# GpSimd takes over loads from SyncE, and two steps move behind the value weights

## The chip, the cores and the metric

One core of one Trainium2 chip. The metric is the device time of one execution in microseconds (us). Engines: TensorE (PE), VectorE (DVE), ScalarE (ACT), GpSimd (POOL), and SyncE (SP), which only issues DMAs. ACT and POOL issue DMAs too, each on a queue of its own. An engine runs its instructions in the order in which they were put on it; one that waits holds all that stand behind it.

## What is computed

One step of a hybrid decoder layer for 2048 prompt tokens and 8 samples of one token each, all in float32, with a width of 1024:

```python
ada = silu(c) @ w_ada + b_ada;  shift, scale, gate = split(ada, 3)
hn = rmsnorm(x, g_norm) * (1 + scale) + shift
xa, za, q, k, v, glr, zg = split(hn @ w_in)           # 5136 columns in all
# RG-LRU group: conv4 over xa, block-diagonal gates, linear recurrence h, y_lru = h * silu(za)
# GLA group, 4 heads, DK 128, DV 256:
log_alpha = log_sigmoid(glr @ w_gla_g2 + b_gla_g2) / 16
S_t = diag(alpha_t) S_{t-1} + k_t^T v_t;  o_t = q_t S_t      # for samples: from state_gla
y_gla = rmsnorm(o) * g_gla_norm * silu(zg)
x = x + gate * (concat(y_lru, y_gla) @ w_out);  y = rmsnorm(x, g_final)
```

Outputs are y for prompt and samples and the new states.

## The kernel before

The prompt is worked in two halves of 1024 tokens; the samples ride with the second half as 8 more columns. Each float32 operand is split into a high and a low part (`hi`, `lo`; `hh`, `hl` for hn), and a product is three matmuls: hi by hi, hi by lo, lo by hi. `hh` and `hl` hold hn transposed, 1024 features on 8 x 128 partitions, for one half at a time.

**hn of the second half.** `modulate` (L187) is called eight times per pair of token tiles, from a list of small steps (`drips`) that the projections of the first half's last tile call between matmuls. Each call turns two k-tiles on PE, scales and shifts the two halves out of PSUM on ACT (L199, L200), rounds on POOL (`hh`, L201) and subtracts on DVE (`hl`, L202). g is the group of 256 tokens, 0 to 3.

**Seven products.** The gates of three heads and two pairs of LRU columns of the second half are made by a Strassen-like scheme with seven products (`seven`, L1517), in the order ZB11, ZT1, ZT2, ZB22, ZT3, ZB21, ZT4. `sums` (L1440) makes their operands out of hn with long DVE steps. To make room, a quarter of hn (the first four k-tiles, second 512 tokens: `a21`, L1437) is overwritten, and kept in DRAM in `a21d`. L1622 loads it back after the last product. The silu of the gates goes to DRAM (`zgd`).

**The heads of the second half.** `gla_head(1, h)` (L1134) runs for h = 3, 0, 1, 2, each followed by one LRU tile:
- `value_weights` (L321) loads two halves of the value weights, in a pool of three places of 1 MB (tag `w`): already split, from `parts` in DRAM (L302), and raw (tag `wr`, two places, L293), because the samples' values use the raw ones.
- `values` (L910): with `sample_values` (L881) first: 64 small matmuls with 8 columns as weights (L889), four copies out of PSUM (L893, to `vs`) and four stores to `vsd` (L896). Then eight token tiles of 24 matmuls (`value_mm`, L335 to L337), each in one of four PSUM places (`acc`). In the first head the 16 low-rank columns ride along, and their transposes wait in the list `turns`; at three entries the oldest is run.
- weights of k and q, also from `parts`, projections (`project`, L650 to L652), the decay, and the chunks of the attention, which are put off by counts of units (`after`, `tick`) and run between the projections.
- `sample_state` (L1055), twice with four samples: loads the samples' values (`vb`, from `vsd`, L1062) and old states (`s0`, L1064) into two places (tag `xt`), scales on ACT (L1068), adds on DVE (L1069); `sample_out` makes the outputs on PE (L1078) and stores the new states (L1079). The normed samples' output `os` goes through PE at L1128.
- `gate_load` (L1165) loads the gates of one segment from `zgd` into `zs` (four places); `finish` uses them (L1131).

Beside this, POOL's queue carries the preparation of the output weights: loads `r` (L806), stores `wd`, `wd2` (L841, L834), whose arithmetic is put on DVE and ACT between other work.

**Who decides the order.** Where the code says `in_order`, the instructions of all engines but SP keep the program's order. Elsewhere the builder puts them on each engine by when they can run by its own reckoning, with the program's order as priority. So SP's issues, and PE's matmuls in `values`, need not follow the program.

Of the kernel before, what the change touches and what calls it, by code (L numbers as in the profile page):

```python
# [8 lines left out]
F32 = mybir.dt.float32  # L9
F32R = mybir.dt.float32r  # L10
I32 = mybir.dt.int32
AF = mybir.ActivationFunctionType
OP = mybir.AluOpType

P = 128
# [4 lines left out]
NS = 8  # L20
H = 4
DK = 128
DV = 256
# [15 lines left out]
HEADS = (3, 0, 1, 2)  # L39
# [10 lines left out]
def dram(ap, off, pattern):  # L50
    return bass.AP(tensor=ap.tensor, offset=ap.offset + off, ap=pattern)
# [3 lines left out]
def hybrid_kernel(ctx, tc, i, o):  # L55
    nc = tc.nc
    V, S, G, PE, SP = nc.vector, nc.scalar, nc.gpsimd, nc.tensor, nc.sync
# [13 lines left out]
    vsd = dpool.tile([H, NS, DV], F32, tag="vsd", name="vsd")  # L71
# [5 lines left out]
    zgd = dpool.tile([8, P, TH + NS], F32, tag="zgd", name="zgd")  # L77
    a21d = dpool.tile([2, P, 4, 512], F32, tag="a21d", name="a21d")
# [32 lines left out]
    Gm = cp.tile([P, KT, 9], F32, name="Gm")  # L111
    Sh = cp.tile([P, KT, 9], F32, name="Sh")
# [74 lines left out]
    def modulate(xt, g, kts):  # L187

        c = slice(g * 256, (g + 1) * 256)
        for k2 in range(kts[0], kts[1], 2):  # L190
            pt = tps().rearrange("p (k t) -> p k t", k=2)
            cg = slice(g % 2 * 256, g % 2 * 256 + 256)
            f = (fs4[(1, 2, 0)[k2 // 4 if g < 2 else 2]][:, k2 % 4:k2 % 4 + 2, cg] if g < 2 or k2 >= 4
                 else ra[k2 // 2][:, :, cg])
            for kt in range(2):
                for j in range(2):
                    PE.transpose(pt[:, kt, j * P:(j + 1) * P],
                                 xt[j][:, (k2 + kt) * P:(k2 + kt + 1) * P], ident)
            S.activation(f[:, 0], pt[:, 0], AF.Identity, scale=Gm[:, k2, 8:9], bias=Sh[:, k2, 8:9])  # L199
            S.activation(f[:, 1], pt[:, 1], AF.Identity, scale=Gm[:, k2 + 1, 8:9], bias=Sh[:, k2 + 1, 8:9])  # L200
            G.tensor_scalar(hh[:, k2:k2 + 2, c], f, 1.0, 0.0, op0=OP.mult, op1=OP.add)  # L201
            V.tensor_tensor(hl[:, k2:k2 + 2, c], f, hh[:, k2:k2 + 2, c].bitcast(F32), op=OP.subtract)  # L202

# [70 lines left out]
    parts = {}  # L274
# [4 lines left out]
    def weights(col, n, k0=0, nk=KT, samples=False, both=None, later=False, pieces=1):  # L279


        q = 48 if n == DV else 0
        c = slice(q, q + nk * n)
        if both is None:
            both = wp.tile([P, 2, 1088], F32R, tag="w", name="w", bufs=3)
        hi, lo = [both[:, j, c].rearrange("p (k n) -> p k n", n=n) for j in range(2)]
        known = (col, k0) in parts
        raw = None
        if samples or not known:
            raw = wp.tile([P, 1088], F32, tag="wr", name="wr")[:, :nk * n].rearrange("p (k n) -> p k n", n=n)  # L290
            for k in range(0, nk, nk // pieces):
                r = slice(k, k + nk // pieces)
                load = lambda r=r: SP.dma_start(raw[:, r], i["w_in"][  # L293
                    0, (k0 + r.start) * P:(k0 + r.stop) * P, col:col + n].rearrange("(k p) n -> p k n", p=P))
                loads.append(load) if k else load()
        split = []
        for k in range(0, nk, nk // pieces):
            r = slice(k, k + nk // pieces)
            split += [lambda r=r: S.copy(hi[:, r], raw[:, r]),
                      lambda r=r: V.tensor_tensor(lo[:, r], raw[:, r], hi[:, r].bitcast(F32), op=OP.subtract)]  # L300
        if known:
            SP.dma_start(both[:, :, c].bitcast(F32), parts[col, k0])  # L302
        else:
            splits.extend(split)
            if not later:
                split_parts()
            parts[col, k0] = dpool.tile([P, 2, nk * n], F32, tag=f"w{col}_{k0}", name="parts")
            stores.append((parts[col, k0], both[:, :, c].bitcast(F32)))
            if not later:
                store_parts()  # L310
        return hi, lo, raw
# [9 lines left out]
    def value_weights(h, samples):  # L321
        n = DV + (RANK if h == HEADS[0] else 0)
        return [weights(V0 + h * DV, n, k0, 4, samples) for k0 in (0, 4)]
# [4 lines left out]
    def drip():  # L328
        if drips:
            drips.pop(0)()  # L330
# [95 lines left out]
    with tc.tile_pool(name="ada", bufs=1, side="right") as ap:  # L426
# [79 lines left out]
        with in_order():  # L506
# [13 lines left out]
            pt = turn(xt0[0:2], (0, 1))  # L520
# [10 lines left out]
            for c in range(1, 4):  # L531
                k = (2 * c, 2 * c + 1)
                if c > 1:
                    ada(c, (0, KT))
                pt = [turn(xt0, (kt,)) for kt in k]
# [345 lines left out]
    def sample_values(h, w, n):  # L881

        n4 = n // 4
        vs = gp.tile([P, DV], F32, tag="os", name="vs")
        ps = acc()
        for kt in range(KT):
            raw = w[kt // 4][2]
            for g in range(4):
                PE.matmul(ps[32 * g:32 * g + NS, :n4], fs[:, kt], raw[:, kt % 4, g * n4:(g + 1) * n4],  # L889
                          start=kt == 0, stop=kt == KT - 1)  # L890
        for g in range(4):
            r = slice(32 * g, 32 * g + NS)
            (S.copy if g % 2 else V.tensor_copy)(vs[r, :min(n4, DV - g * n4)], ps[r, :min(n4, DV - g * n4)])  # L893
        for g in range(4):
            c = slice(g * n4, min((g + 1) * n4, DV))
            G.dma_start(vsd[h][:, c], vs[32 * g:32 * g + NS, :c.stop - c.start])  # L896
        if n > DV:
            r = slice(96, 96 + NS)
            return low_rank(ps[r, DV - 3 * n4:n4], r, TH)
        return lambda: None  # L900
# [9 lines left out]
    def values(half, h, w):  # L910
        first = h == HEADS[0]
        n = DV + (RANK if first else 0)
        vh, vl = new_values()
        turns = [sample_values(h, w, n)] if half == 1 else []
        for tt in range(8):
            if tt == 4:
                while drips:
                    drip()
            c = slice(tt * P, (tt + 1) * P)
            ps = acc()  # L920
            value_mm(ps[:, :n], c, w, n, (0, KT))
            hi, lo = vh[tt // 4][:, tt % 4], vl[tt // 4][:, tt % 4]
            S.copy(hi, ps[:, :DV])  # L923
            V.tensor_tensor(lo, ps[:, :DV], hi.bitcast(F32), op=OP.subtract)  # L924
            if len(turns) == 3 or tt == 7 and turns:
                turns.pop(0)()
            if first:
                turns.append(low_rank(ps[:, DV:n], slice(0, P), tt * P))
            tick(0.5)
        for f in turns:  # L930
            after(1, f, True)
        return vh, vl
# [122 lines left out]
    def sample_state(h, smp, b0, st, done):  # L1055

        if b0 == 0:
            st[:] = [cp.tile([P, NS, 32], F32, tag="sc", name="qm"), gp.tile([P, DV], F32, tag="os", name="os")]
            V.memset(st[0], 0.0)
        qm = st[0]  # L1060
        vb = xp.tile([P, 4, DV], F32, tag="xt", name="xt")
        SP.dma_start(vb, dram(vsd, (h * NS + b0) * DV, [[0, P], [DV, 4], [1, DV]]))  # L1062
        s0 = xp.tile([P, 4, DV], F32, tag="xt", name="xt")
        SP.dma_start(s0, i["state_gla"][0, b0:b0 + 4, h].rearrange("b k v -> k b v"))  # L1064
        for n in range(4):
            b = b0 + n
            V.tensor_copy(qm[:, b, b:b + 1], smp[:, 0, b:b + 1])
            S.activation(s0[:, n], s0[:, n], AF.Copy, scale=smp[:, 2, b:b + 1])  # L1068
            V.scalar_tensor_tensor(s0[:, n], vb[:, n], smp[:, 1, b:b + 1], s0[:, n],  # L1069
                                   op0=OP.mult, op1=OP.add)  # L1070
        after(3, lambda: sample_out(h, b0, st, s0, done), True)
# [62 lines left out]
    def gla_head(half, h, wv=None):  # L1134
        ns = len(SEGS[half])
        if wv:
            wk, wq = wkq0
            v, prep0, rest = first_head()
        else:
            v = values(half, h, value_weights(h, half == 1))  # L1140
            wk = weights(K0 + h * DK, DK)
            wq = weights(Q0 + h * DK, DK)
        prep, zs, os_, state = {}, {}, [None], []
# [21 lines left out]
        def gate_load(s):  # L1165
            c0, n = SEGS[half][s]
            for dt in range(2):
                z = new_zs()
                SP.dma_start(z[:, :n], zgd[2 * h + dt][:, c0:c0 + n])
                zs[s, dt] = z[:, :n]  # L1170

        def finish(s):
# [264 lines left out]
    def a21():  # L1437
        return [(hh, hl)[u][:, :4, 512:TH] for u in range(2)]
# [180 lines left out]
        gates_seven(1 + n)  # L1619
    while drips:  # L1620
        drip()
    for u, x in enumerate(a21()):  # L1622
        SP.dma_start(x.bitcast(F32), a21d[u])
    close_sp()
    for k, h in enumerate(HEADS):
        gla_head(1, h)
# [282 lines left out]
    for x in pairs[:2]:  # L1909
        x.new(A11)  # L1910
        r = wp.tile([P, 1088], F32, tag="wr", name="wr")[:, :D].rearrange("p (q k t) -> p q k t", q=2, k=4)
# [214 lines left out]
    for n in range(2, 16):  # L2126
        g = n - 1
# [17 lines left out]
    for q in range(8):  # L2145
        g, k = 2 + q // 2, q % 2
# [63 lines left out]
```

## Time and profile before

| | us |
|---|---|
| runs | 1469.28, 1469.33, 1471.35 |
| median | 1469.33 |
| profiled execution | 1468.39 |
| its span, first to last instruction | 1466.6 |

| engine | busy us | share |
|---|---|---|
| PE | 1428.5 | 97% |
| DVE | 1049.6 | 72% |
| ACT | 690.0 | 47% |
| POOL | 188.7 | 13% |

Times in rows are us from the span's start. hn of the second half is made from about 560 to 603, the seven products run from about 602 to 710, the heads of the second half from 710 to about 1090, then LRU tiles and, to the end, the output projection. A row of a timeline has start, duration, engine, line, operation, tiles written and read, shape, count, and in brackets the idle time of the engine ahead of it with what ended it; of a row with a count it is the first of the merged ones. SPq and ACTq are DMA issues of SP and ACT. A row of waits has who waited for what, total us, times, longest.

### The profile page before, as it was taken

To read this page: it belongs to the slowest core of one execution; us is meant where nothing else is said; L and a number is where in the kernel's file an instruction comes from. 1 tells how busy PE (TensorE), PEld (TensorE's weight loads), DVE (VectorE), ACT (ScalarE), POOL (GpSimd) and SP (SyncE) were. 2 spreads that over 40 slices of the span, in tenths; PEclk is the share of its full clock that TensorE was granted. 3 is DMA by queue.
4 is the path that set the end of the run, shared out by engine and by line. 5 is a ranking of instruction groups with operands and counts; after the bars stand their busy time and mean duration, and the time that the engine had idled before them with its cause. 6 is when DMAs were issued, how large, how long until landed. Compare 5 with 4: busy or idle time off the path is not lost.

```text
span 1466.6 us, 23589 instructions
## 1 busy us (share of the span) xinstructions
PE 1428.5 (97%) x8741; PEld 1254.4 (86%) x8741; DVE 1049.6 (72%) x2473; ACT 690.0 (47%) x1255; POOL 188.7 (13%) x316
## 2 busy tenths in 40 slices
PE   8999999999999999999999899999999999999998
PEld 6888988899898988788899899999998887778886
DVE  5757657776666778845458678586778986688886
ACT  4653544652445467624353454534557622144342
POOL 1200111212121121100102222222100000000000
PEclk9999999999999999999999999999999999999999
DMA  9755876765656455657836746567353757693453
GB/s 331 259 183 176 272 243 214 255 213 184 202 197 219 127 192 196 225 194 247 313 107 202 244 151 196 181 207 256 130 201 104 277 200 266 251 360 122 139 177 115
DMA packets 169944, 305.33 MB, mean 208 GB/s; under 512 B 12962, under 2 KB 102722, under 8 KB 167389
## 3 DMA queue, kind: packets, MB, share of 16 engines
q1 hardware_dynamic: 119029, 233.21, 47.0%
q0 software_dynamic: 17888, 53.56, 10.4%
q10 hardware_dynamic: 32912, 17.04, 3.8%
q8 instruction: 69, 1.13, 0.3%
q14 instruction: 46, 0.38, 0.1%
HBM read 188.51 MB, written 115.33 MB: 207 GB/s over the span
## 4 chain that ended last, share of the span: by engine, by line
PE 76%; DVE 8%; DMA 6%; ACT 5%; issue 5%; POOL 1%; SPq 0%; ACTq 0%; DVEq 0%; POOLq 0%
PE acc L1797 12%; PE acc L650 10%; PE acc L651 10%; PE acc L652 10%; PE tp L1797 9%; PE acc L1511 6%; PE acc L335 3%; PE acc L336 3%; PE acc L337 3%; DMA w<-parts 2%; PE po L1040 1%; DMA mixd<-zs 1%; PE acc L1271 1%; PE tp L1126 1%; PE acc L1273 1%
## 5 line engine op out<-in xcount | busy, mean ns | idle before, releaser
L650 PE MATMUL acc<-hh,w 128*128 128x512 f32 (+3 forms) x1112 | 386.9, 348 | 6.5 <-DMA w<-parts 5.4
L651 PE MATMUL acc<-hl,w 128*128 128x512 f32 (+3 forms) x1112 | 376.4, 338 | 0.0
L652 PE MATMUL acc<-hh,w 128*128 128x512 f32 (+3 forms) x1112 | 375.9, 338 | 0.0
L650 PEld LDWEIGHTS acc<-hh,w 128*128 128x128 f32 x1112 | 209.8, 189 | 25.1 <-DVE e L985 3.6
L651 PEld LDWEIGHTS acc<-hl,w 128*128 128x128 f32 x1112 | 209.9, 189 | 17.9 <-issue 1.2
L652 PEld LDWEIGHTS acc<-hh,w 128*128 128x128 f32 x1112 | 209.7, 189 | 16.3
L1797 PE MATMUL acc<-w,a 128*128 128x512 f32 (+1 forms) x792 | 184.8, 387 | 0.0
L1797 PEld LDWEIGHTS acc<-w,a 128*128 128x128 f32 x792 | 146.8, 188 | 33.2 <-issue 3.4
L335 PE MATMUL acc<-w,hh 128*128 128x256 f32 (+1 forms) x508 | 145.5, 286 | 4.9 <-DMA w<-parts 3.1
L337 PE MATMUL acc<-w,hl 128*128 128x256 f32 (+1 forms) x508 | 143.4, 282 | 0.0
L336 PE MATMUL acc<-w,hh 128*128 128x256 f32 (+1 forms) x508 | 143.3, 282 | 0.0
L1797 PE MATMUL tp<-w,a 128*128 128x512 f32 x564 | 136.0, 391 | 0.0
L1797 PEld LDWEIGHTS tp<-w,a 128*128 128x128 f32 x564 | 105.3, 188 | 26.8 <-issue 5.1
L335 PEld LDWEIGHTS acc<-w,hh 128*128 128x128 f32 x508 | 96.3, 190 | 7.4 <-DMA w<-parts 3.3
L337 PEld LDWEIGHTS acc<-w,hl 128*128 128x128 f32 x508 | 96.7, 190 | 0.0
L336 PEld LDWEIGHTS acc<-w,hh 128*128 128x128 f32 x508 | 96.2, 189 | 0.1
L1092 ACT ACTIVATE zs<-acc 128x512 f32<-128x512 f32 (+3 forms) x71 | 34.7, 488 | 107.7 <-PE acc L652 97.4
L1647 ACT CAST a<-s 128x512 fp32r<-128x512 f32 x61 | 36.5, 620 | 96.0 <-issue 36.7
L1234 DVE SCALAR_TENSOR_TENSOR cv<-xa,vecT,cv 128x512 f32<-128x512 f32 (+2 forms) x120 | 76.3, 639 | 7.0 <-ACT cv L1232 6.5
L1093 DVE SCALAR_TENSOR_TENSOR zs<-zs,acc 128x512 f32<-128x512 f32 (+3 forms) x71 | 38.9, 548 | 46.4 <-ACT zs L1092 46.4
L923 ACT CAST vh<-acc 128x256 fp32r<-128x256 f32 x56 | 20.7, 371 | 89.4 <-PE acc L337 74.0
L924 DVE TENSOR_TENSOR vl<-acc,vh 128x256 fp32r<-128x256 f32 x56 | 23.2, 421 | 51.5 <-ACT vh L923 51.2
(393 smaller groups left out, 2721.5 us busy)
## 6 DMA issues: line engine op xcount, KB each, us to landing
parts<-w SPq DMA_DIRECT2D x37, 1024.0 KB
w<-parts SPq DMA_DIRECT2D x28, 1024.0 KB
wr<-in_w_in_dram SPq DMA_DIRECT2D x44, 512.0 KB
a<-mixd SPq DMA_DIRECT2D x63, 256.0 KB
w<-wd SPq DMA_DIRECT2D x12, 1024.0 KB
w<-twd SPq DMA_DIRECT2D x20, 512.0 KB
mixd<-zs ACTq DMA_DIRECT2D x34, 256.0 KB
wada<-in_w_ada_dram SPq DMA_DIRECT2D x16, 512.0 KB
```

Source lines behind the costliest of these rows:

```text
L335: PE.matmul(ps, hh[:, kt, c], hi[:, kt % 4], start=kt == 0, stop=False)
L336: PE.matmul(ps, hh[:, kt, c], lo[:, kt % 4], start=False, stop=False)
L337: PE.matmul(ps, hl[:, kt, c], hi[:, kt % 4], start=False, stop=kt == KT - 1)
L650: PE.matmul(ps[:, :n], hi[:, kt], a, start=kt == 0, stop=False)
L651: PE.matmul(ps[:, :n], hi[:, kt], b, start=False, stop=False)
L652: PE.matmul(ps[:, :n], lo[:, kt], a, start=False, stop=kt == KT - 1)
L1092: S.activation(z, ps, AF.Tanh, scale=0.5)
L1093: V.scalar_tensor_tensor(z, z, 1.0, ps, op0=OP.add, op1=OP.mult)
L1234: V.scalar_tensor_tensor(cv[:, cq], xa[:, cq.start + k:cq.stop + k], cw[k], cv[:, cq], op0=OP.mult, op1=OP.add)
L1511: PE.matmul(ps, w[:, u, k], x[v][k], start=start and (k, u, v) == (0, 0, 0), stop=(k, u) == (3, 1), skip_group_check=True)
L1647: S.copy(t[:, 0, k], (low(t) if src is None else src)[:, k])
L1797: PE.matmul(ps, t[:, u, k], w[:, v, k, c], start=(q < 3 or ps is own) and (k, u, v) == (0, 0, 0), stop=(k, u) == (3, 1), skip_group_check= ...
```

## The change

- `modulate`: for g of 2 and 3 the second of the two activations out of PSUM is a `tensor_scalar` on DVE.
- `weights`: where the split weights lie in DRAM already, their load comes first in the program, and the raw weights' loads are issued by POOL.
- `values`: `sample_values` is called after four token tiles, not ahead of the first; `turns` is emptied down to two entries each time.
- `sample_state` and `gate_load`: their three loads are issued by POOL.
- The loads of `a21d` stand behind those of the first head's value weights.

```diff
@@ modulate
             S.activation(f[:, 0], pt[:, 0], AF.Identity, scale=Gm[:, k2, 8:9], bias=Sh[:, k2, 8:9])
-            S.activation(f[:, 1], pt[:, 1], AF.Identity, scale=Gm[:, k2 + 1, 8:9], bias=Sh[:, k2 + 1, 8:9])
+            if g < 2:
+                S.activation(f[:, 1], pt[:, 1], AF.Identity, scale=Gm[:, k2 + 1, 8:9], bias=Sh[:, k2 + 1, 8:9])
+            else:
+                V.tensor_scalar(f[:, 1], pt[:, 1], Gm[:, k2 + 1, 8:9], Sh[:, k2 + 1, 8:9], op0=OP.mult, op1=OP.add)
@@ weights
         raw = None
+        if known:
+            SP.dma_start(both[:, :, c].bitcast(F32), parts[col, k0])
         if samples or not known:
...
-                load = lambda r=r: SP.dma_start(raw[:, r], i["w_in"][
+                load = lambda r=r: (G if known else SP).dma_start(raw[:, r], i["w_in"][
                     0, (k0 + r.start) * P:(k0 + r.stop) * P, col:col + n].rearrange("(k p) n -> p k n", p=P))
...
-        if known:
-            SP.dma_start(both[:, :, c].bitcast(F32), parts[col, k0])
-        else:
+        if not known:
             splits.extend(split)
@@ values
-        turns = [sample_values(h, w, n)] if half == 1 else []
+        turns = []
         for tt in range(8):
             if tt == 4:
                 while drips:
                     drip()
+                if half == 1:
+                    turns.append(sample_values(h, w, n))
...
-            if len(turns) == 3 or tt == 7 and turns:
+            while len(turns) >= 3:
+                turns.pop(0)()
+            if tt == 7 and turns:
                 turns.pop(0)()
@@ sample_state
-        SP.dma_start(vb, dram(vsd, (h * NS + b0) * DV, [[0, P], [DV, 4], [1, DV]]))
+        G.dma_start(vb, dram(vsd, (h * NS + b0) * DV, [[0, P], [DV, 4], [1, DV]]))
         s0 = xp.tile([P, 4, DV], F32, tag="xt", name="xt")
-        SP.dma_start(s0, i["state_gla"][0, b0:b0 + 4, h].rearrange("b k v -> k b v"))
+        G.dma_start(s0, i["state_gla"][0, b0:b0 + 4, h].rearrange("b k v -> k b v"))
@@ gla_head
-            v = values(half, h, value_weights(h, half == 1))
+            w = value_weights(h, half == 1)
+            if half and h == HEADS[0]:
+                for u, x in enumerate(a21()):
+                    SP.dma_start(x.bitcast(F32), a21d[u])
+            v = values(half, h, w)
@@ gate_load
-                SP.dma_start(z[:, :n], zgd[2 * h + dt][:, c0:c0 + n])
+                G.dma_start(z[:, :n], zgd[2 * h + dt][:, c0:c0 + n])
@@ hybrid_kernel, ahead of the second half's heads
-    for u, x in enumerate(a21()):
-        SP.dma_start(x.bitcast(F32), a21d[u])
     close_sp()
```

## The prediction

> **What bounds the kernel now.** I read the page first, then the waits of TensorE (PE), then timelines and stretches around each wait that the diff can reach.
>
> ```profile
> PE 1428.5 (97%) x8741; PEld 1254.4 (86%) x8741; DVE 1049.6 (72%) x2473; ACT 690.0 (47%) x1255; POOL 188.7 (13%) x316
> ```
>
> PE is busy for 97% of the span, so an edit that leaves PE's own work as it is can gain only from PE's idle time. The diff leaves PE's matmuls as they are: it moves the samples' 64 small ones, and removes none. GpSimd (POOL) has room: 13%. The waits of PE between 690 and 1110 us, where the second half's heads run, longest first:
>
> ```profile
> PE acc L650 <- DMA w<-parts: 5.4, 2, 3.3
> PE acc L335 <- DMA w<-parts: 3.1, 1, 3.1
> PE acc L1271 <- ACT tx L1274: 2.4, 1, 2.4
> PE tp L1128 <- DVE os L1088: 2.3, 2, 1.5
> PE acc L335 <- ACT vs L893: 1.5, 1, 1.5
> ```
>
> And in the stage before them, where hn of the second half is made and the sums for the seven products begin:
>
> ```profile
> PE acc L1511 <- DVE zs L1093: 1.5, 1, 1.5
> PE acc L1511 <- DVE so L1449: 1.2, 1, 1.2
> ```
>
> Weights that arrive late cost 8.5 us in three waits, samples' values that leave PSUM late 1.5, late sample outputs 2.3, VectorE (DVE) 2.7. These are what the diff can win or make longer. A long wait costs more than itself. The stretches:
>
> ```profile
> 600.00:620.00 20.00, 17.67 (x75) 13.33 (x73) 20.00 (x21) 10.39 (x13) 1.54 (x2) 1.00 0.66 213
> 716.00:719.40 3.40, 0.29 (x4) 0.08 (x2) 0.68 (x4) 0.40 (x2) 3.09 (x6) 1.00 0.99 398
> 719.40:723.00 3.60, 3.60 (x17) 3.60 (x18) 0.34 (x1) 0.37 (x1) 1.45 (x2) 0.54 1.07 374
> 820.00:832.00 12.00, 12.00 (x107) 12.00 (x106) 5.58 (x17) 1.61 (x5) 5.26 (x9) 1.00 0.84 259
> 832.00:840.00 8.00, 4.68 (x27) 4.39 (x26) 5.49 (x15) 5.60 (x9) 0.16 (x1) 0.95 0.95 327
> 931.60:935.00 3.40, 3.01 (x17) 3.04 (x18) 2.34 (x6) 1.40 (x3) 1.57 (x3) 1.00 0.82 324
> ```
>
> The columns are the stretch, its length, the busy time of PE, weight load, DVE, ScalarE (ACT) and POOL, the granted clock, the DMA share and GB/s. After the 3.1 us wait the clock is 0.54 for 3.6 us, so that wait costs another 3.6 x 0.46 = 1.7. The shorter of the two L650 waits (5.4 - 3.3 = 2.1) ended at about 932, and the clock after it is 1.00. So between 2.1 and 3.1 us of idling lies the point from which 1.7 us more are due. [...]
>
> **The change part by part.** Durations are of the profiled execution (1468.39 us, its span 1466.6); the median shown is 1469.33, 0.94 above, and I carry the sum to it unchanged.
>
> *modulate: for g of 2 and 3 the second activation goes from ACT to DVE.* The last but one of the eight calls:
>
> ```profile
> 594.52 0.55 ACT L199 ACTIVATE fs<-tp,Sh,Gm 128x256 f32<-128x256 f32 x1
> 594.97 1.23 ACT L1281 ACTIVATE tg<-tg,lc 128x1024 f32<-128x1024 f32 x1
> 596.11 0.55 ACT L200 ACTIVATE fs<-tp,Sh,Gm 128x256 f32<-128x256 f32 x1
> ```
> ```profile
> 596.81 0.62 POOL L201 TENSOR_SCALAR hh<-fs 128x512 fp32r<-128x512 f32 x1 [3.83 <-ACT fs L200]
> ```
> ```profile
> 597.46 0.69 DVE L202 TENSOR_TENSOR hl<-fs,hh 128x512 fp32r<-128x512 f32 x1 [2.62 <-POOL hh L201]
> ```
>
> The first half is ready at 595.1, the second only at 596.7, because ACT does other work between them; DVE idles 2.62 us for it. The same operation on DVE stands in the trace once:
>
> ```profile
> L237 DVE TENSOR_SCALAR hnf<-tp,Gm,Sh x2: 544/544/545, 16.0 to 17.2; 128x256 f32<-128x256 f32 x2
> ```
>
> Eight of these are 4.4 us of DVE and take 8 x 0.55 = 4.4 from ACT. Here the second half would be done inside DVE's idle 2.62, POOL would start at about 595.2, and L202 at about 595.9: 1.5 us sooner, with the last call's 0.54 also done in the hole. From there DVE is the bound (busy 20.00 of 20.00 between 600 and 620), and PE waits for it 1.5 + 1.2 us. So DVE's lead reaches PE: 1.5 at most; 0.55 if DVE's next step waits for ACT, whose queue has lost one L200 of 0.55 there; a loss of up to 0.5 if an added operation lands on the full stretch. I take 1.3, nearer to the upper end, since the other seven holes of one call also shrink. **-1.3.** Next in line is DVE itself.
>
> *Samples' values behind four tiles.* The three non-first heads take their samples' matmuls while outputs of the head before are still pending, so the copies out of PSUM (L893) come late; in the last head a value tile waits 1.5 us for that bank. Four tiles later no such work is pending, and the wait goes. What is late next there is the query weights, below. **-1.5**, between -1.7 with the restart and 0 if the copies wait for something else. In the first head the samples also hold one of the four acc banks:
>
> ```profile
> 709.91 1.13 PE L889 MATMUL acc<-wr,fs 128*8 128x68 f32 x64
> ```
> ```profile
> 714.50 0.39 PE L335 MATMUL acc<-w,hh 128*128 128x272 f32 x1 [0.24 <-DVE zq L1093]
> ```
>
> The third tile's first half (714.50 to 716) is the last thing PE can do before the 3.1 us wait. With the samples gone a fourth tile's first half, 1.5 us, goes ahead of the wait in place of 1.1. **-0.4**, between -0.4 and +1.1.
>
> *hn's spilled part (a21d) behind the value weights; value weights before the raw ones; raw ones on POOL.* SP's issues:
>
> ```profile
> 700.57 0.32 SPq L302 DMA_DIRECT2D w<-parts  x1
> 700.94 0.43 SPq L293 DMA_DIRECT2D wr<-in_w_in_dram  x1
> 704.58 0.53 SPq L1623 DMA_DIRECT2D hh<-a21d  x1
> 705.16 0.71 SPq L1623 DMA_DIRECT2D hl<-a21d  x1
> 707.29 0.33 SPq L302 DMA_DIRECT2D w<-parts  x1
> ```
>
> In the program the a21d loads stand ahead of all the others, yet they are issued after two of them: SP's order is that in which places come free, not the program's. The a21d loads wait for the third to last product of the last seven (ZT3), the second value weights for a w buffer that the product after it (ZB21) frees. Moving the lines does not alter which is free first, so I expect a21d still at about 704.6, ahead of the weights on the same queue, and the 3.1 us wait with its 1.7 to stay. The DMA engines are full there (share 0.99 and 1.07), so a raw load on another queue changes little: **0**.
>
> *Query weights (L650's waits).* For the second head:
>
> ```profile
> 807.55 0.94 SPq L293 DMA_DIRECT2D wr<-in_w_in_dram  x2
> ...
> 819.49 0.32 SPq L1062 DMA_DIRECT2D xt<-vsd  x1
> 819.90 0.38 SPq L1064 DMA_DIRECT2D xt<-in_state_gla_dram  x1
> 827.38 4.08 SPq L1169 DMA_DIRECT2D zs<-zgd  x3
> 831.55 1.19 SPq L302 DMA_DIRECT2D w<-parts  x2
> ```
>
> The weights leave at 831.55 when the value tiles free a buffer, so an emptier SP does not bring them forward: 0 from SP's relief. If POOL's queue had bandwidth of its own, the last two gates (zs) would no longer stand in front of them: 0.39 MB by their shapes, 1.2 us at 327 GB/s in each of two heads, -2.4. [...] I keep **0**; the other side is the second rival.
>
> *Samples' states and gates on POOL.* The last head's chain has no slack:
>
> ```profile
> 1075.04 0.38 SPq L1064 DMA_DIRECT2D xt<-in_state_gla_dram  x1
> ```
> ```profile
> 1079.99 1.71 ACT L1068 ACTIVATE xt<-xt,smp 128x256 f32<-128x256 f32 x4 [5.27 <-DMA xt<-in_state_gla_dram]
> ```
> ```profile
> 1082.32 0.64 PE L1078 MATMUL po<-xt,qm 128*32 128x256 f32 x8
> ```
> ```profile
> w<-parts SPq DMA_DIRECT2D x28, 1024.0 KB
> wr<-in_w_in_dram SPq DMA_DIRECT2D x44, 512.0 KB
> ...
> out_dram<-xt POOLq DMA_DIRECT2D x8, 512.0 KB, 5.5
> ```
>
> From SP the 512 KB take 4.95 us to their reader, ACT is held for 5.27, and everything behind it on ACT waits. POOL's 512 KB transfers of the same tile land after 5.5 (median), 0.55 more, and PE's wait for os grows by that: **+0.5**, between 0 and +3 (three heads with a chain like it, and POOL held by an older store). The gates' waits inside 827.38's 4.08 us would hold POOL instead of SP, and with it samples' values, stores of the output weights and their next loads; those are used many us later, so 0; without that cover up to 4.
>
> The sum is -1.3 - 1.5 - 0.4 + 0.5 = -2.7: 1465.7 for the profiled execution, **1466.6** for the median, just inside 0.2% (2.9 us), which is about what a measurement of this kernel can tell from no change.
>
> **The rivals.** *First: a21d does go behind the second value weights.* For it: the lines are moved, and both are issued within 2.7 us. Against it: the order by readiness above. The 2 MB would no longer stand in front, the wait of 3.1 and its 1.7 go: 1466.6 - 4.8 = 1461.8.
>
> *Second, slower: next loads collide with the query weights.* The samples' matmuls end four tiles later, about 11 us, so what hangs on them moves too: the next head's two raw loads (1 MB, now at 807.55, in an easy stretch) and the samples' own two (1 MB, now at 819.5). They would fall between 820 and 835, where the share is already 0.84 and then 0.95, and the query weights are issued at 831.55. It decides once 1 MB of it is in transit at that moment: 1 MB at 327 GB/s is 3.2 us later, in the second and the third head (the last loads no raw weights ahead), and the 2.1 us wait grows past the point of the clock: 2 x 3.2 + 1.7 = 8.1, so 1474.7. For it: the shares. Against it: the stretch 820 to 832 still has room for about 0.7 MB, and weights have a queue to themselves.
>
> *Third: the gains do not arrive.* DVE's added work fills the hole without a lead, and the copies of L893 wait elsewhere: about 0 with the +0.5, so 1469.8.
>
> **How the numbers follow.** The forecast has 0.42; its terms' bounds spread it over faster 0.19, same 0.19, slower 0.04. The first rival 0.18, all faster. The second 0.27: slower 0.25, same 0.02. The third 0.13: faster 0.05, same 0.04, slower 0.04. Together faster 0.42, same 0.25, slower 0.33. The range runs from just below the first rival, 1460.5, to just above the second, 1475, with no more than 2 in 10 outside. The forecast's own range is 1464.5 to 1469.5.
>
> **What would show it.** DVE's hole before L202 at about 595 is gone, and PE's two waits at L1511 are shorter by 1 to 1.5 in sum. No wait of L335 for L893. SP still issues a21d ahead of the second value weights, and L335's wait for w<-parts stays near 3 us with a clock near 0.5 behind it; if a21d is issued later and the wait is gone, the first rival holds. L650's waits for w<-parts stay at 5.4 in two places; if they are 10 or more, the second holds. ACT's waits for the states grow by about half a us each. I am wrong if a new wait of PE appears that hangs on POOL's queue, such as gates or output weights that come late.

## The result: slower by 2 us, and the profile after

| kernel | median us | lowest to highest | executions |
|---|---|---|---|
| before, same chip | 1471.66 | 1468.40 to 1475.67 | 12 |
| changed | 1474.17 | 1469.34 to 1476.91 | 12 |

The ratio is 1.0014, with a 95% interval from 1.0000 to 1.0028: +2.1 us by the ratio, +2.5 by the medians, where the forecast said -2.7. The interval begins at no change, so this run alone shows little more than that the gain is not there. The profiled execution took 1472.66, its span 1470.9 (before: 1466.6). Lines of the changed kernel stand 3 to 11 higher than before: L653 to L655 are the projections that were L650 to L652, L338 to L340 the value matmuls, L1522 the seven products.

The page's first part. PE is as full as it was, GpSimd fuller:

```profile
PE 1431.4 (97%) x8741; PEld 1257.5 (85%) x8741; DVE 1053.5 (72%) x2481; ACT 687.5 (47%) x1247; POOL 218.8 (15%) x364
```

PE's waits between 690 and 1110 us (line, releaser: total, times, longest):

```profile
PE acc L653 <- DVE r L830: 3.7, 1, 3.7
PE acc L653 <- DMA w<-parts: 3.5, 2, 2.1
PE tp L1135 <- DVE os L1095: 2.7, 4, 1.1
PE acc L338 <- DMA w<-parts: 2.3, 1, 2.3
```

The value tile's wait for the samples' copy (1.5) is gone; the first head's wait is 2.3 (was 3.1). The key and query weights are waited for in three heads: 1.4, 3.7 and 2.1 (were 3.3, 2.1 and 0.7). The one of 3.7 is put down to another releaser (`r`), as is the 0.7 of before (`f`). But in each of the two the matmul starts 0.14 us after the last piece of the weights has landed (930.89 and 931.03; 1022.92 and 1023.06), as it does where the wait is named `w<-parts` (839.37 and 839.51 in before), so both are waits for weights.

PE's waits between 575 and 625 us:

```profile
PE tp L197 <- DVE ra L203: 3.1, 2, 2.6
PE acc L1522 <- DVE so L1460: 1.2, 1, 1.2
PE acc L1522 <- DVE ra L1460: 1.0, 1, 1.0
```

The sums are waited for 2.2 us (were 2.7), but the turned tiles, whose release has moved to DVE (L203), 3.1 (were 2.5, released by ACT):

```profile
PE tp L197 <- ACT ra L200: 2.5, 1, 2.5
```

**A ledger by stage.** All kernels here have 8741 matmuls, so the start of PE's matmul number 3500, 4000 and so on gives each stage's length (to some 0.3 us, since a few matmuls change places). "First" and "second head" here are the first and second that are worked, and a second profile of the same kernel is called "again". In the first profile of before: matmul 3500 at 556 us, 4000 at 659, 4500 at 745 (end of the first head's values), 5250 at 849, 6000 at 950, 6750 at 1049, 8500 at 1408. Differences from that profile in us:

| kernel, profile | hn, sums 3500-4000 | products, first values -4500 | second head -5250 | third -6000 | last -6750 | behind -8500 |
|---|---|---|---|---|---|---|
| before, again | +1.1 | -0.1 | -0.1 | -0.2 | +1.3 | +0.9 |
| changed | +1.9 | -1.3 | -3.0 | +4.7 | +2.3 | +0.2 |
| modulate's part alone | +1.7 | +1.1 | +0.1 | -0.3 | +1.6 | +1.3 |
| changed without modulate's part | 0.0 | -1.2 | -3.3 | +4.8 | +2.2 | -0.4 |
| ... raw weights pinned | 0.0 | -1.3 | -3.0 | +4.8 | +1.4 | -0.3 |
| ... and states held back | +1.1 | -1.4 | -2.3 | -1.2 | +4.3 | -1.0 |
| the same, again | 0.0 | -1.3 | -2.4 | -1.5 | +1.0 | -0.4 |

So the changed kernel lost in hn and in the third and last head, and won in the first and second. Two questions follow: what modulate's part costs, and what moved the weights' waits.

### The profile page after: what moved, and what is told of

It is laid out like the page before. It is cut to its first block, busy times and chain, and to the rows that moved or that the text cites. A ratio compares the mean times of both kernels' runs of the same rounds, so it can differ in the third digit from the quotient of the medians.

```text
span 1470.9 us, 23571 instructions
## 1 busy us (share of the span) xinstructions
PE 1431.4 (97%) x8741; PEld 1257.5 (85%) x8741; DVE 1053.5 (72%) x2481; ACT 687.5 (47%) x1247; POOL 218.8 (15%) x364
## 5 line engine op out<-in xcount | busy, mean ns | idle before, releaser
L653 PE MATMUL acc<-hh,w 128*128 128x512 f32 (+3 forms) x1112 | 388.7, 350 | 7.3 <-DVE r L830 3.7
L655 PE MATMUL acc<-hh,w 128*128 128x512 f32 (+3 forms) x1112 | 377.6, 340 | 0.0
L653 PEld LDWEIGHTS acc<-hh,w 128*128 128x128 f32 x1112 | 211.6, 190 | 25.6 <-DVE r L830 3.9
L655 PEld LDWEIGHTS acc<-hh,w 128*128 128x128 f32 x1112 | 211.4, 190 | 16.3
L338 PE MATMUL acc<-w,hh 128*128 128x256 f32 (+1 forms) x508 | 145.4, 286 | 2.4 <-DMA w<-parts 2.3
L340 PE MATMUL acc<-w,hl 128*128 128x256 f32 (+1 forms) x508 | 143.6, 283 | 0.2 <-DVE hl L228 0.2
L338 PEld LDWEIGHTS acc<-w,hh 128*128 128x128 f32 x508 | 96.3, 190 | 4.3 <-DMA w<-parts 2.5
L340 PEld LDWEIGHTS acc<-w,hl 128*128 128x128 f32 x508 | 96.8, 190 | 0.4 <-DVE hl L228 0.4
```

Source lines behind the costliest of these rows:

```text
L338: PE.matmul(ps, hh[:, kt, c], hi[:, kt % 4], start=kt == 0, stop=False)
L340: PE.matmul(ps, hl[:, kt, c], hi[:, kt % 4], start=False, stop=kt == KT - 1)
L653: PE.matmul(ps[:, :n], hi[:, kt], a, start=kt == 0, stop=False)
L655: PE.matmul(ps[:, :n], lo[:, kt], a, start=False, stop=kt == KT - 1)
```

## Experiments: modulate

**The part alone, and the changed kernel without it.** The first adds these lines to the kernel before, the second takes them out of the changed kernel (`...`, here and below: code left out).

```
+            if g < 2:
+                S.activation(f[:, 1], pt[:, 1], ...)
+            else:
+                V.tensor_scalar(f[:, 1], pt[:, 1], ...)
```

> The kernel before with one part of the change alone: modulate's second activation on DVE for g of 2 and 3. Collision theory (the changed kernel loses because the samples' next loads, moved four token tiles later, run beside the key and query weights of the third and the last head): nothing is moved there, so 1471.7 as the kernel before, within 1.5 either way, and key-weight waits of 5.4 us in two places. Modulate theory (the changed kernel loses in the hn stage, where PE is 2.9 us later at 600 us than at 580): the whole loss of the hn stage stands here, 1471.7 + 2.4 = 1474.1, with a PE wait of 2.6 us or more in front of L197 and a clock below 1 behind it. Chance theory (the restart of the clock comes and goes by itself): within 1 us of the kernel before.

> The changed kernel without one part: modulate's second activation on ACT again. Collision theory: 1474.2, within 1 us, key-weight waits as in the changed kernel (7 us in three places). Modulate theory: 1474.2 - 2.4 = 1471.8, PE no later at 600 us than the kernel before.

The part alone took 1475.52 against 1471.47, ratio 1.0028 (1.0019 to 1.0037). The changed kernel without it took 1472.22, ratio 1.0004 (0.9994 to 1.0014). So modulate's part alone costs 4.1 us by the ratio, clear of noise. Taken out of the changed kernel it is worth 1.5 (1.0014 to 1.0004), and there the two intervals overlap; all other parts together (+0.6) cannot be told from no change. The mechanism shows in the timelines of the changed kernel, DVE and GpSimd, 589 to 593 us:

```profile
589.12 0.69 DVE L205 TENSOR_TENSOR hl<-fs,hh 128x512 fp32r<-128x512 f32 x1 [0.48 <-POOL hh L204]
589.73 0.54 DVE L203 TENSOR_SCALAR fs<-tp,Gm,Sh 128x256 f32<-128x256 f32 x1
591.07 0.69 DVE L205 TENSOR_TENSOR hl<-fs,hh 128x512 fp32r<-128x512 f32 x1 [0.81 <-POOL hh L204]
591.68 0.54 DVE L203 TENSOR_SCALAR ra<-tp,Gm,Sh 128x256 f32<-128x256 f32 x1
```
```profile
590.42 0.62 POOL L204 TENSOR_SCALAR hh<-fs 128x512 fp32r<-128x512 f32 x1 [1.34 <-DVE fs L203]
592.37 0.62 POOL L204 TENSOR_SCALAR hh<-ra 128x512 fp32r<-128x512 f32 x1 [1.34 <-DVE ra L203]
```

Each L203 stands on DVE behind the L205 of the call before, which waits for GpSimd's L204, which waits for the L203 before it: a loop over two engines of 1.95 us a call. In the kernel before, where ACT makes both halves, the calls come in pairs, 3.25 us apart, 1.6 a call:

```profile
588.56 0.69 DVE L202 TENSOR_TENSOR hl<-fs,hh 128x512 fp32r<-128x512 f32 x1 [1.44 <-POOL hh L201]
591.81 0.69 DVE L202 TENSOR_TENSOR hl<-ra,hh 128x512 fp32r<-128x512 f32 x1 [1.36 <-POOL hh L201]
```

The tile in PSUM is held until L203 has read it, so PE turns the last call's tiles later:

```profile
592.38 0.27 PE L197 MATMUL tp<-ident,xst 128*128 128x128 f32 x1
```
```profile
594.23 0.33 PE L197 MATMUL tp<-ident,xst 128*128 128x128 f32 x1 [0.47 <-DVE ra L203]
```

The first is before, the second the changed kernel, 1.85 us later. Only the 0.47 of the wait belongs to the loop: the tiles of the call ahead are 1.22 late already (593.16, before 591.94), and from 585 to 592 PE was busy throughout, at a mean clock of 0.76. Such a slow clock comes and goes in kernels with ACT as well (last section). The profile of the part alone, with a clock of 1.00 there, shows the loop without it, with a wait of 1.30 and the tile 2.34 later than before:

```profile
594.72 0.33 PE L197 MATMUL tp<-ident,xst 128*128 128x128 f32 x1 [1.30 <-DVE ra L203]
```

**The subtraction behind the next call's activation.**

```
-            V.tensor_tensor(hl[...], f, hh[...], op=OP.subtract)
+            while rests:
+                with behind(V):
+                    rests.pop()()
+            rests.append(lambda: V.tensor_tensor(hl[...], f, hh[...], op=OP.subtract))
+            if g < 2 or k2 == 6:
+                rests.pop()()
```

> Modulate's part alone as in the first run, but with the subtraction of one call queued on VectorE behind the activation of the next call (within each g). Loop theory: the chain is cut, tp banks come free as early as with ACT, the loss of 2.6 at 600 us goes: 1471.5 or up to 1.3 below. Load theory: the same work is on VectorE, so 1475 as in the first run.

The waits of the turned tiles in the run with the part alone, and then the waits of this run, 575 to 630 us:

```profile
PE tp L197 <- DVE ra L203: 3.9, 3, 2.4
```
```profile
PE tp L199 <- DVE ra L205: 2.4, 1, 2.4
PE acc L1521 <- DVE so L1459: 1.2, 1, 1.2
PE acc L1521 <- DVE ra L1459: 1.0, 1, 1.0
```

Two of the three waits are gone and the stage is 0.6 us shorter than before (it was 1.7 longer), both with a clock of 1.00 there: the loop is what lengthened it. But the median was 1475.73 against 1471.34, ratio 1.0024 (1.0006 to 1.0042). The stage's loss went, the kernel's did not.

**DVE in the last two calls alone** (`if g < 3 or k2 < 4` for ACT).

> The kernel before with VectorE's activation in the last two calls of modulate alone (g of 3, k2 of 4 and 6), where VectorE had its hole of 2.62 us. Loop theory (with all eight calls on VectorE each call's activation waits in VectorE's queue behind the subtraction of the call before, which waits for GpSimd, which waits for the activation before: 1.95 us a call, and the tp banks come free late): two calls at the end make no such chain for PE, the hole is filled: 1471.5 - 1.0 = 1470.5, PE not later at 600 us than the kernel before. Load theory (VectorE is full between 600 and 620, and each added operation of 0.54 stands there): 1471.5 + 1.0 = 1472.5.

1472.88 against 1471.34, ratio 1.0016 (1.0002 to 1.0030), its stage 0.4 us longer. The promised gain did not come; if anything it is a loss. Two waits for the sums (L1514 for `so`) were 2.8 in total, about what before has (2.7): filling DVE's hole gave PE nothing. DVE begins its first long step of the sums at 596.47 (598.18 before), but the last call's subtraction now stands behind that step, and the next step of the sums begins only at 599.94 (600.47): most of the lead is spent on DVE itself.

**The same three on a quieter kernel.** With the states held back (next section, 1465.74) executions of one kernel scatter less (1464.44 to 1467.59).

> The kernel with the states held back until the query weights have landed, and modulate's part added as the change has it, on all eight calls. There the spread from the heads is small (1464.4 to 1467.6), so the price of that part alone shows. Loop theory: what its own stage lost, 2.0, and no more: 1465.7 + 2.0 = 1467.7. If DVE in modulate also costs some 2.4 behind its stage, as the swapped order did here (1468.1 against 1465.7): 1465.7 + 4.4 = 1470.1.

> As the run before it, with modulate's part put back in the order of the run with the subtraction behind the next activation. If the swapped order wins 0.6 us in its stage and nothing else follows from it: 0.6 below that run. If a kernel with VectorE in modulate loses 3 us behind that stage, as that run's median said and its trace did not: 3 above.

> As the run before it, with VectorE in the last two calls of modulate alone. Loop theory: 1465.7, within 0.7, or up to 1.0 below. If any use of VectorE there costs 2.4 behind the stage: 1468.1.

Ratios to before: 0.9965 (0.9952 to 0.9979) without, 0.9989 (0.9979 to 1.0000; 1469.51) with all eight calls, 0.9978 (0.9965 to 0.9992; 1468.14) swapped, 0.9968 (0.9956 to 0.9981; 1467.44) with the last two. All eight cost 3.5 us by the ratios, the swapped order 1.9, the last two nothing that can be told. The interval with all eight only touches the one without; that of the swapped order overlaps both, so how much of the cost the swap saves is not told.

**More profiles** of two of these kernels, all eight calls on DVE (twice) and none (once), to find the part outside of the stage.

> The kernel with the states held back and all eight calls on VectorE once more, for another profile: its median lies 3.8 us above the same kernel without VectorE in modulate, yet its profiled execution (1466.8) was 2.7 us below its own median. If the missing time is a slow clock behind the waits of the hn stage and of the sums, the stretch from 575 to 650 us is 3 us or more longer than in the kernel without; if it lies in the heads, this stretch is 2 us longer at most and the rest is behind 700 us.

> The same kernel, for a third profile, with the same two possibilities: 3 us or more between 575 and 650 us, or 2 at most there and the rest in the heads.

> The kernel with the states held back and modulate on ScalarE once more, for a second profile: no wait of the third head for weights, and a stretch from 575 to 650 us as in the kernel before or 1.1 us longer, by whether the clock falls behind the 2.5 us wait of the turned tiles.

The times of these single executions were 1471.92, 1470.65 and 1463.88 (the kernel before, once beside them: 1474.28). Over all profiles taken here, the stage of hn and sums is 1.7 to 2.3 us longer than in the first profile of before wherever DVE has all eight calls (six profiles, mean 1.9), and 0 to 1.3 where ACT has them (ten, mean 0.5). That is 1.4 us. The slow clock behind the wait for the turned tiles stands in four of the six and in four of the ten; without it the stage is 1.7 and 2.3 longer against 0 to 0.2, with it 1.7 to 2.0 against 1.1 to 1.3. With the last two calls alone the stage was 0.4 longer without it and 1.8 with it. The stretch behind matmul 6750 is +1.2 on the mean of the same six, from -1.1 to +3.6, and -0.2 on that of the ten, from -1.0 to +0.9: another 1.4 us, with the two swapped profiles at +1.5 and +2.0. In the changed kernel's own profile it was only +0.2. Together about 2.8; the kernels' times say 1.5 to 4. Why a stretch 450 us later becomes longer is open: with this part and without it, the instructions of every engine stand in the same order except around 600 us. The mean of the six rests on the two further profiles with this part (+3.6 and +3.2); the other four alone have a mean of 0.0. In those two PE starts the sample outputs (`po`) 1.7 and 1.8 us late with no releaser to be seen; the first also waits 0.9 for the splitting of the output weights on DVE, and in the second the clock is 0.51 for 7 us behind a wait of 3.4 at 1110. The first profile of that same kernel has `po` 1.1 late and the stretch 0.3 shorter. No run shows the cause.

## Experiments: the weights' waits

**Late values and loads on GpSimd, one without the other.** Together with the two kernels that stand already they make a table of four, all without modulate's part.

```
-        turns = [sample_values(h, w, n)] if half == 1 else []
+        turns = []
...
+                if half == 1:          # at tt == 4
+                    turns.append(sample_values(h, w, n))
```

> The kernel before with one part alone: the samples' values behind four token tiles, all loads still on SP. Collision theory: raw weights and samples' states still move some 11 to 14 us later and meet the key weights, now on the same queue, where they stand ahead of the weights or behind them: 1471.7 + 4 = 1475.7, key-weight waits of 9 us or more in sum over three heads, with a clock near 0.5 behind at least one. Modulate theory: 1471.7 - 1.5 = 1470.2, since the wait of a value tile for the samples' copy (1.5) goes and nothing else happens.

> The changed kernel without modulate's part and with the samples' values ahead of the first token tile: what is left is the loads on GpSimd and the order of the value weights. With the kernel before (1471.5), the late values alone (1487.2) and the changed kernel without modulate's part (1472.2) it fills a table of four. If the parts simply add, moving the loads is worth -15 and this one is 1456.5. If the queue matters only where values are late (on SP the samples' loads then stand ahead of the key weights), it is within 2 us of the kernel before: 1471.5 to 1473.5, with the value tile's wait for the samples' copy still there.

In the right column the order of the value weights and of `a21d` is that of the change, too.

| median us (ratio to before) | loads on SP | loads on GpSimd |
|---|---|---|
| values ahead of the tiles | 1471.4 | 1473.19 (1.0015, 0.9998 to 1.0031) |
| values behind four tiles | 1487.23 (1.0107, 1.0092 to 1.0121) | 1472.22 (1.0004, 0.9994 to 1.0014) |

The parts do not add. Late values alone cost 15.8 us, four times the 4 that the collision theory had for them, and moving the loads, which by itself wins nothing, takes that back.

**The changed kernel with the samples' values early again.**

> The changed kernel without one part: the samples' values ahead of the first token tile again, loads on GpSimd as changed. Collision theory: raw weights and states are loaded at the old times, so 1474.2 - 4 = 1470, key-weight waits of 5 us or less in sum, a value tile's wait of 1.5 for the samples' copy back in the last head. Modulate theory: 1474.2 + 1.5 = 1475.7.

1475.42, ratio 1.0032 (1.0017 to 1.0047). The value tile's wait for `vs` was back with 2.6 us. Against the changed kernel (1.0014) late values are worth some 2.6 us by the ratios, once the loads are on GpSimd, though the intervals overlap; the collision theory, which had them as the loss, failed here.

**The states alone back on SP** (`G.dma_start` to `SP.dma_start` for `vb` and `s0`; no modulate part).

> The changed kernel without modulate's part and with the samples' states back on SP; raw weights and gates stay on GpSimd, values stay late. Queue theory (late values cost 15 us with all loads on SP because the load of the samples' values, vb, waits on SP for their store to land, with the key weights behind it): the key-weight waits are 15 us or more in sum, 1484 or more. Order theory (raw weights and gates ahead of the key weights did it): 7 us in sum as on GpSimd, 1472.

1492.55, ratio 1.0141 (1.0119 to 1.0164). SP's waits, 690 to 1120 us, and its issues before the second head's projections:

```profile
SPq L1066 <- DMA vsd<-vs: 87.0, 6, 25.8
```
```profile
835.60 0.32 SPq L1066 DMA_DIRECT2D xt<-vsd  x1
836.01 0.39 SPq L1068 DMA_DIRECT2D xt<-in_state_gla_dram  x1
836.49 1.38 SPq L290 DMA_DIRECT2D w<-parts  x2
```

The load of `vb` waits on SP for the stores of `vs` to land, 87 us in six waits, and the key weights stand behind it: they leave at 836.49, and PE waits 10.5 us for them there, 24.9 in three heads. So with raw weights and gates on GpSimd, late values cannot do without the move of the states. With all loads on SP (22.0 in three heads) SP's waits for those stores are only 18.0 in five (9.4 in the kernel before), beside 77.9 for the gates' loads (69.8 before); the key weights stand behind both, and how the 15.8 divides between them is not shown.

**Raw weights of the later heads pinned early on GpSimd's queue** (no modulate part).

```
+                if known and col != V0 + HEADS[0] * DV:
+                    with behind(G):
+                        load()
```

> The changed kernel without modulate's part, with the raw value weights of the three later heads queued on GpSimd behind everything the head before gave that queue: they leave near 803, 900 and 996 instead of between 820 and 832, 910 and 919. Collision theory (1 MB of raw weights and 1 MB of states run beside the key weights): the third head's key-weight wait falls from 3.9 and a slow clock (2.6) behind it to 2 or less without it, the last head's stays: 1472.2 - 4 = 1468. Buffer theory (the key weights are late because the value tiles free their buffer late): 1472, the wait of 3.9 unchanged.

1469.82 against 1471.34, ratio 0.9991 (0.9978 to 1.0004). The third head's wait did not fall: 4.9 (the longest of these two; it was 3.7).

```profile
PE acc L654 <- DMA w<-parts: 7.4, 2, 4.9
```
```profile
920.15 0.54 POOL L1070 DMA_DIRECT2D xt<-vsd  x1 [0.29 <-issue]
920.68 0.77 POOL L1072 DMA_DIRECT2D xt<-in_state_gla_dram  x1
```
```profile
920.36 1.88 SPq L290 DMA_DIRECT2D w<-parts  x2
```

The states (1 MB) leave in the same half microsecond as the weights, here 0.2 us ahead of them (in the changed kernel 0.7 behind: 922.36, 921.69). In the second head of this kernel they leave 2.5 us after the weights (832.49 and 830.02), and PE waits 1.0 there. That wait is put down to `mid` on DVE, but again the weights' last piece lands 0.14 us before the matmul starts (836.54 and 836.68).

**The states held back until the query weights have landed**, with the raw weights pinned.

```
+        if b0 == 0:
+            G.tensor_scalar(vb[:, 0, :2], wq[0][:, KT - 1, :2].bitcast(F32), 1.0, 0.0, ...)
         G.dma_start(vb, ...)
...
+        with behind(G):
+            G.dma_start(s0, ...)
```

> As the run with the raw weights pinned, and the samples' first four states and values (1 MB a head) leave GpSimd only once the second of the two late weights (the query weights) has landed, which a copy of two columns of them into the destination sees to. State theory (it is this 1 MB, issued within half a us of the key weights in the third head, that shares the engines with them; the raw weights were not it): the third head's wait of 4.9 falls to 1.5 or less and the slow clock behind it (1.7) goes, the second head's stays at nothing, the last head's at 2.5: 1469.8 - 5 = 1465. Traffic theory (other transfers, the stores of output weights among them, keep the engines full there anyway): within 1.5 us of 1469.8, the wait still above 3.

**1465.74** (1464.44 to 1467.59) against 1471.38, ratio **0.9965** (0.9952 to 0.9979): faster than both kernels, -5.2 us. GpSimd's queue in the third head; the weights left at 921.67:

```profile
926.86 0.18 POOL L1071 TENSOR_SCALAR xt<-w 128x2 f32<-128x2 f32 x1 [0.94 <-DMA w<-parts]
927.30 0.59 POOL L838 DMA_DIRECT2D wd<-p  x1 [0.27 <-issue]
927.89 0.54 POOL L1072 DMA_DIRECT2D xt<-vsd  x1
928.57 0.76 POOL L1075 DMA_DIRECT2D xt<-in_state_gla_dram  x1
```

For key or query weights PE waits in this profile in the last head and, put down to `f` on DVE (the weights land at 837.48, the matmul starts at 837.62), in the second:

```profile
PE acc L654 <- DMA w<-parts: 2.7, 1, 2.7
PE acc L654 <- DVE f L977: 1.1, 1, 1.1
```

In the third there is no such wait. The stretch from 920 to 932 us has PE busy for all 12.00 us; the ledger's third head goes from +4.8 to -1.2 and -1.5.

**The hold without the pin.**

> The changed kernel without modulate's part, with the states held back until the query weights have landed, and the raw weights not pinned. State theory: the states alone made the third head's wait; the raw weights that leave beside the key weights cost less than 2 us: 1465.7 to 1467.7. If the raw weights carry as much as the states (512 KB of them leave beside the key weights): 1469 or more, with a wait of 2.5 or more in the third head.

1467.55, ratio 0.9968 (0.9956 to 0.9981). The third head waits 3.0 for weights that left at 920.35; one of the two raw loads left with them:

```profile
920.40 0.76 POOL L295 DMA_DIRECT2D wr<-in_w_in_dram  x1 [0.16 <-PE acc L337]
```

So each of the two makes a wait by itself, and both have to be out of the way for it to go. By time the pin is worth 0.4 us by the ratios and 1.8 by the medians, with intervals that overlap.

**The kernel before against itself.**

> The kernel before once more, for a second profile of it and for what two kernels that are the same differ by here: ratio 1.000 within 0.0015. The profile of before was of an execution 3 us below that kernel's median; if such spread sits in the waits for weights (first head, second, third, last), they are 2 to 4 us longer in sum here, and the stage from 575 to 660 us takes the same time within 0.3.

1470.18 against 1471.38, ratio 0.9993 (0.9980 to 1.0007). Its profile is 3.2 us longer than the first: 1.1 in hn, where nothing differs but the clock, 1.3 in the last head, 0.9 behind. So in this pair one profile's ledger is good to about 1.3 us a stage. Other profiles of one kernel differ by up to 1.5 up to the third head, but by 3.3 in the last head (+4.3 and +1.0, states held back) and by 3.9 behind it (-0.3 and +3.6, the same with modulate's part). The +4.7 of the third head is far outside of that; the last head's +2.3 and the +0.2 behind are not.

## Why the prediction was wrong, step by step

- **modulate (-1.3).** This step failed, sign included. The prediction read one hole, the 2.62 us before the seventh call, and took the other seven to shrink too. It asked what DVE waits for, not what the new operation would be queued behind: on DVE each L203 stands behind a subtraction that hangs on GpSimd. The runs put 1.5 to 4 us there, about 1.4 of it in the stage itself and the rest not explained (in the changed kernel's own ledger +1.9 and +0.2). The observation named for it came half: the waits for the sums fell by 0.5, and a longer one for the turned tiles (L197) took their place. The hole did go (0.36 is left of the 2.62, ahead of L205 at 597.78). Filling only the hole that was read (the last two calls) won nothing, so "DVE's lead reaches PE" was wrong too.
- **Samples' values behind four tiles (-1.5).** Right in mechanism: L338 has no wait for `vs`. With the loads on GpSimd it is worth 1.6 to 2.6 by the ratios (1.0015 to 1.0004 without modulate's part, 1.0032 to 1.0014 with it), neither clear of noise. But it was costed as a part by itself; with the loads on SP it is +15.8.
- **First head (-0.4).** Too small: over all profiles that stage is 1.2 to 3.0 us shorter with late values, and with early values from 0.1 shorter to 2.3 longer.
- **a21d's order (0).** Half right. SP's issues in the changed kernel:

```profile
706.05 0.53 SPq L1150 DMA_DIRECT2D hh<-a21d  x1
708.73 0.32 SPq L293 DMA_DIRECT2D w<-parts  x1
709.10 0.53 SPq L1150 DMA_DIRECT2D hl<-a21d  x1
```

The first megabyte still goes ahead of the second value weights, by readiness; the second now goes behind them. The wait was 2.3, between the forecast's 3.1 and the first rival's none.
- **Key and query weights (0), and the second rival (+8.1).** The second step that failed: the 0. Without modulate's part the other terms add up to -1.4, and that kernel measured +0.6 (-0.9 to +2.1 by its interval): in its ledger the 4.5 us won up to the end of the second head are more than lost again in the third and the last (4.8 and 2.2). The rival had the mechanism, and the wrong heads and size. Raw weights and states did move onto the weights, in the third head: POOL and SP in the changed kernel.

```profile
921.61 0.76 POOL L298 DMA_DIRECT2D wr<-in_w_in_dram  x1 [0.45 <-DMA vsd<-vs]
922.36 0.54 POOL L1069 DMA_DIRECT2D xt<-vsd  x1
922.91 0.76 POOL L1071 DMA_DIRECT2D xt<-in_state_gla_dram  x1
```
```profile
921.69 1.88 SPq L293 DMA_DIRECT2D w<-parts  x2
```

That head lost 4.7 (3.2 + 1.7 had been reckoned for a head), the last 2.3; in the second all of them except one raw load leave 2.3 us or more behind the weights (833.27 to 835.16, the weights at 830.95), and it won 3.0. Over three heads the sum of these waits was 7.2, not the 10 named as the rival's sign. The time came close to the rival's 1474.7 for another reason. Whether GpSimd's queue has bandwidth of its own, which decides between the 0 and the -2.4, no run shows by itself. What the runs showed: with 1 MB on that queue beside the weights on SP's, PE waited 4.9 us in the third head (DMA share 0.92 from 920 to 931), and with that 1 MB held back not at all (0.85 from 920 to 932).
- **States on GpSimd (+0.5).** Wrong in sign: ACT's waits for the states, before and after, 690 to 1110 us:

```profile
ACT xt L1068 <- DMA xt<-in_state_gla_dram: 14.7, 4, 5.3
```
```profile
ACT xt L1075 <- DMA xt<-in_state_gla_dram: 5.0, 4, 3.1
```

The wait for the sample outputs (`os`) grew by 0.4 all the same (2.3 to 2.7), but that goes with the late values: it is 1.9 with the loads on GpSimd and the values early, and 3.0 with late values and the loads on SP. No wait of PE hangs on the gates.
- **The base.** The sum was made against a profiled execution of 1468.39, 3 us below the median of the 12 executions measured with the changed kernel. Its stages were taken as fixed; the second profile shows 1.1 us of clock in hn alone.

## What to carry to other kernels

Before giving an engine a step of a chain that it already ends, write down what the new instruction is queued behind: two engines that hand one tile back and forth need the next tile's first step ahead of this tile's last (here the stage was 0.6 us shorter than before with that order, and 1.7 longer without it). When late work moves later, list the transfers that it releases and the time at which each leaves, head by head, against the transfer that PE will wait for next; with 1 MB that left in the same microsecond PE waited 4.9 us, and holding it back by one small dependency won 3.8 us by the ratios (0.9991 to 0.9965). Price parts that share a queue together: here one was worth -1.6, or +15.8, by whether the other was there.

## What the runs showed of the hardware

The prediction put the point at which a wait slows the clock between 2.1 and 3.1 us. It is not a matter of length alone. The stretch behind the 2.5 us wait of the turned tiles, in the first and the second profile of before (columns as in the prediction, the clock third from the end):

```profile
584.40:588.00 3.60, 3.52 (x30) 3.53 (x31) 1.72 (x3) 2.47 (x8) 1.35 (x3) 1.00 0.10 36
```
```profile
584.80:588.60 3.80, 3.75 (x21) 3.75 (x21) 1.72 (x3) 2.38 (x6) 1.59 (x3) 0.57 0.10 35
```

One kernel, one wait, a clock of 1.00 or of 0.57, worth 1.1 us of its stage; among the ten profiles with that wait on ACT four had it. Taken over the slow stretch alone, the clock of the second is 0.50 for 3.4 us (584.7 to 588.1), and 1.00 behind it. Behind the changed kernel's 2.3 us wait in the first head it was 0.65 for 4.7 us, which is again 0.50 for 3.4 (718.6 to 722.0), and behind its 3.7 us wait:

```profile
931.00:937.00 6.00, 5.97 (x19) 6.00 (x20) 0.81 (x2) 0.40 (x1) 2.03 (x4) 0.50 0.83 328
```

Here half speed lasts twice as long (0.50 from 930.2 to 937.0, 6.8 us), a loss of 3.0 (half of PE's 5.97 in the row) where the prediction had reckoned 1.7. So waits of 2.3 and 2.5 us, too, had a slow clock behind them here, the one of 2.5 in some executions only; what decides it was not shown.
